# A two-layer conv/attention trunk: one depthwise block moved to VectorE, norms and opening loads reordered

## The chip, the cores and the metric

The kernel runs on one core of one Trainium2 chip. The metric is the device time of one execution in microseconds (us). A core has TensorE (matrix products; its weight loads are shown as an engine of their own), VectorE, ScalarE, GpSimd (POOL) and SyncE (SP, which here only issues DMAs). Each engine works off its own queue in order and waits on semaphores for the others.

## The reference, cut to what matters

The input is 256 tokens of 1024 channels, float32. Two layers, each with a mixer between two half-step SwiGLU FFNs: the first layer's mixer is a causal Conformer convolution, the second's a stick-breaking attention. The change sits in the first FFN's opening and in the convolution.

```python
for i in range(DEPTH):                       # 2
    x = x + 0.5 * swiglu_ffn(rms_norm(x, g[0]), ffn_w_in[i, 0], ffn_w_out[i, 0])
    h = rms_norm(x, g[1])
    x = x + (conformer_conv(h, ...) if i == 0 else stick_breaking_attention(h, ...))
    x = x + 0.5 * swiglu_ffn(rms_norm(x, g[2]), ffn_w_in[i, 1], ffn_w_out[i, 1])
return rms_norm(x, final_g)

def conformer_conv(h, ...):
    val, gate = jnp.split(h @ w_pw1 + b_pw1, 2, axis=-1)
    u = val * jax.nn.sigmoid(gate)
    u = depthwise_causal_conv(u, w_dw) + b_dw          # 31 taps, each channel by itself
    u = jax.nn.silu(layer_norm(u, ln_g, ln_b))
    return u @ w_pw2 + b_pw2
```

## The kernel before, in words

**Tiling.** The 256 tokens are two tiles of 128 (t = 0, 1); the 1024 channels are eight blocks of 128 (k = 0 to 7). Every float32 product is made of three products of two parts: an operand is split into hi (a cast by ScalarE, L142) and lo (the difference, a tensor_tensor on VectorE, L143), and `mm3` (L171) multiplies hi by hi, hi by lo and lo by hi. All weights are loaded from memory once, into one of three `raw` buffers, and split into one of six `hi` and six `lo` buffers of `ring`. A load waits until its `raw` buffer has been split; a split waits until TensorE has finished with the buffer that it takes.

**FFN** (`ffn`, L257). Eleven steps j of 256 hidden columns. Each loads a piece of `w_in` and of `w_out`. In the first FFN the first two steps (`lead` = 2) are done by `start` (L766), written out by hand; from step j = 2 on `C` (L281) makes the products with the tokens as columns, and `V` (L303) multiplies the step's result by `w_out`, one step later. Outside the stages written out by hand a planner sets the order on each engine, by estimated readiness.

**The opening** (`start`, L798 to L849) is in hand-written order for TensorE, SP, ScalarE and VectorE. SP loads x, then `w_in` for j = 0 and 1. `keep_busy` issues dummy transposes on TensorE. `turn_x`, `gain` and `split_x` bring x into the operand layout, `cast(j, k)` splits one row block of the weights (`lo` on VectorE, or on POOL where `nc.gpsimd` is passed), `mm` issues the products. After it the planner takes over; SP fetches `w_out` for j = 0 and j = 1 before `w_in` for j = 2, in the order of the loop at L352.

**The convolution** (`conv`, L385 to L611) is in hand-written order too.
- `U(e, t)` (L426) makes 24 products for the column pair e (blocks 2e and 2e + 1, value and gate) of token tile t. After its third step (k = 2) it runs `finish()`, the gate that the U before it left pending, and then what else it was given. At its end ScalarE scales the result into `vg` (L434).
- The pending gate (L436) transposes `vg` on TensorE (L439), and for each of its two blocks ScalarE takes a sigmoid (L442) and VectorE multiplies (`up`, L443). Then `shifted` (L468) issues four DMAs for the block, which make four copies shifted by one token each (`sk`).
- `weights(e)` (L454) builds the tap matrices of two blocks on VectorE, one instruction for each.
- `taps(k, tb, nt)` (L478) does the 31 taps of block k as 32 small matrix products on `sk` (64 instructions in the trace), with `finish()` in the middle; ScalarE then adds the bias into `acc[k]` (L490).
- `norm_in(t, q)` (L496) transposes four blocks of `acc` back and takes `bn_stats`; `norm(t)` (L506) makes the layer norm and the SiLU of one token tile: VectorE, POOL (rstd), VectorE, ScalarE (sigmoid), VectorE, for two halves. `turn(t, q)` (L525) transposes the result and splits it; `out_mm(t, n)` (L533) makes 24 products with `conv_w_pw2`.
- The order is L552 to L610. In the second half all taps of tile 0 are followed by those of tile 1; `norm(0)` lies between the taps of tile 1, `norm(1)` behind out_mm's first products.

Of the kernel before, what the change touches and what calls it, by code (L numbers as in the profile page):

```python
# [14 lines left out]
P = 128  # L15
# [17 lines left out]
def trunk_kernel(  # L33
# [55 lines left out]


# [8 lines left out]
    def load_conv_consts():  # L99
# [121 lines left out]
    def u_mm(t, units, between=None):  # L221
        ps = ps_u.tile([P, 512], F32, tag="u", name=nm("psu"))
        for k in range(KD):
            u_step(ps, t, k, units)
            if between is not None and k == 2:
                between()
        return ps

    def u_cm(units):
# [10 lines left out]
        u = wk.tile([P, T, P], F32, tag="A", bufs=13, name=nm("u"))  # L240
# [4 lines left out]
    def row_rstd(hTs):  # L245

        pr = ps_t.tile([P, T, P], F32, tag="tr", name=nm("pr"))
        for t in range(T):
            rb = wk.tile([P, P], F32, tag="A", bufs=13, name=nm("rb"))
# [7 lines left out]
    def ffn(i, f, gi, hTs, next_gi, first=None, start=None, hook=None, final=False):  # L257
# [3 lines left out]
        def gate(t, j, ps):  # L261
            rstd = hTs[t][2]
            s = wk.tile([P, 256], F32, tag="A", bufs=13, name=nm("s"))
            nc.scalar.activation(s, ps[:, 0:256], AF.Sigmoid, scale=rstd)
            p = wk.tile([P, 256], F32, tag="A", bufs=13, name=nm("p"))
            nc.vector.scalar_tensor_tensor(p, ps[:, 0:256], rstd, s, op0=ALU.mult, op1=ALU.mult)
            a = wk.tile([P, 256], F32, tag="A", bufs=13, name=nm("a"))
# [13 lines left out]
        def C(j, units, rrow):  # L281

            hs, ls = [], []
            for q in range(2):
                for c in range(2):
                    u = u_cm([w[:, :, c, q * P : (q + 1) * P] for w in unit] for unit in units)
                    if c == 0:
                        nc.vector.tensor_tensor(u, u, rrow, op=ALU.mult)  # L288
                        a = wk.tile([P, T, P], F32, tag="A", bufs=13, name=nm("s"))
# [60 lines left out]
        outs = [None, None]  # L350
        prev = None
        for j in range(NJ):  # L352
# [4 lines left out]
            vu = load_rows(w_out, 2 * j)  # L357
# [10 lines left out]
            if j == NJ - 1:  # L368
                V(0, j - 1, prev)
                V(1, j - 1, prev, (0,))  # L370
                V(0, j, vu)
                outs[0] = end(0)
                V(1, j - 1, prev, (1,))
                V(1, j, vu)
                outs[1] = end(1)
            elif j:
                for t in range(T):
                    V(t, j - 1, prev)
            prev = vu
# [5 lines left out]
    def conv(hTs, next_gi, next_w):  # L385
# [40 lines left out]
        def U(e, t, *todo):  # L426
# [5 lines left out]
            ps = u_mm(t, units[e], between=between)  # L432
# [3 lines left out]
            def gate():  # L436
# [3 lines left out]
                for q, k in enumerate((2 * e, 2 * e + 1)):  # L440
# [8 lines left out]
                    elif t == T - 1:  # L449
                        shifted(k, 0, SW)  # L450
# [17 lines left out]
        def shifted(k, a, b):  # L468

            if k not in sks:  # L470
                sks[k] = wk.tile([P, 4, SW], F32, tag="sk", bufs=4, name=nm("sk"))
            for g in range(4):
                v = up[k][32 * g : 32 * g + 32, a:b]
                nc.sync.dma_start(
# [3 lines left out]
        def taps(k, tb, nt, pool, tag):  # L478
# [13 lines left out]
            )  # L492

# [39 lines left out]
        def out_mm(t, n):  # L533
            ns = slice(n * 512, (n + 1) * 512)
            pv = ps_v.tile([P, 512], F32, tag=f"v{t}{n}", name=nm("psv"))
            for k in range(KD):
# [4 lines left out]
                )  # L541
            nc.vector.tensor_tensor(xt[t][:, ns], pv, xt[t][:, ns], op=ALU.add)

        for _ in range(KD):
            up.append(wk.tile([P, H + T * P], F32, tag="A", bufs=13, name=nm("up")))
# [5 lines left out]
        with tc.manual_schedule(engines={E.PE, E.SP, E.Activation, E.DVE}):  # L551
# [11 lines left out]
            U(1, 0, (weights, 0), (cast, units[2][0]))  # L563
# [50 lines left out]
    def attention(hTs, next_gi):  # L614
# [9 lines left out]
        ones = wk.tile([P, WS], F32, tag="sk", bufs=4, name="ones")  # L624
# [260 lines left out]
```

## Time and profile before

| | |
|---|---|
| median of 3 runs | 998.3 us (998.02 to 998.73) |
| the profiled execution | 1000.22 us, of which the span from its first to its last instruction is 998.4 us |
| TensorE busy | 983.9 us, 99% of the span |
| VectorE busy | 709.2 us, 71% |
| ScalarE busy | 514.5 us, 52% |
| POOL busy | 134.8 us, 14% |
| the chain that ended last | TensorE 93%, VectorE 3%, ScalarE 2% |

TensorE's share is an average over all stages. What is to be read from it is only where TensorE is not busy, and who was waited for there. Times in the rows are microseconds from the span's start.

### The profile page before, as it was taken

To read this page: it belongs to the slowest core of one execution; us is meant where nothing else is said; L and a number is where in the kernel's file an instruction comes from. 1 tells how busy PE (TensorE), PEld (TensorE's weight loads), DVE (VectorE), ACT (ScalarE), POOL (GpSimd) and SP (SyncE) were. 2 spreads that over 40 slices of the span, in tenths; PEclk is the share of its full clock that TensorE was granted. 3 is DMA by queue.
4 is the path that set the end of the run, shared out by engine and by line. 5 is a ranking of instruction groups with operands and counts; after the bars stand their busy time and mean duration, and the time that the engine had idled before them with its cause. 6 is when DMAs were issued, how large, how long until landed. Compare 5 with 4: busy or idle time off the path is not lost.

```text
span 998.4 us, 14842 instructions
## 1 busy us (share of the span) xinstructions
PE 983.9 (99%) x5727; PEld 817.7 (82%) x5727; DVE 709.2 (71%) x1092; ACT 514.5 (52%) x872; POOL 134.8 (14%) x169
## 2 busy tenths in 40 slices
PE   9999999999989999999999999999999999999997
PEld 7788888886778888888888888888777788888885
DVE  5876776754777776767777676767777986767654
ACT  6654545353536454545554545455554355555532
POOL 3011111100011111111121111111101011111111
PEclk9999999999999999999999999999999999999999
DMA  7867564536735756565557464755625255656511
GB/s 254 293 218 247 179 223 154 169 105 225 220 123 174 229 169 211 166 213 162 176 170 225 154 222 158 217 163 169 210 90 166 91 163 169 212 168 210 170 43 43
DMA packets 143175, 177.76 MB, mean 178 GB/s; under 512 B 6456, under 2 KB 126336, under 8 KB 143104
## 3 DMA queue, kind: packets, MB, share of 16 engines
q1 hardware_dynamic: 142752, 176.26, 54.9%
q8 instruction: 45, 0.74, 0.3%
q10 hardware_dynamic: 352, 0.55, 0.2%
q14 instruction: 26, 0.21, 0.1%
HBM read 171.08 MB, written 1.05 MB: 172 GB/s over the span
## 4 chain that ended last, share of the span: by engine, by line
PE 93%; DVE 3%; ACT 2%; issue 1%; DMA 1%; POOL 0%; POOLq 0%; SPq 0%; ACTq 0%; DVEq 0%
PE psc L236 28%; PE psc L237 16%; PE psv L172 8%; PE psv L173 8%; PE psv L174 8%; PE psc L239 4%; PE psu L172 4%; PE psu L173 4%; PE psu L174 4%; PE pc L484 2%; DVE lo L143 1%; PE ptr L194 1%; PE pz L662 1%; ACT hi L142 1%; PE pwo L172 1%
## 5 line engine op out<-in xcount | busy, mean ns | idle before, releaser
L143 DVE TENSOR_TENSOR lo<-raw,hi 128x1024 fp32r<-128x1024 f32 (+1 forms) x358 | 397.3, 1133 | 81.8 <-ACT hi L142 81.4
L236 PE MATMUL psc<-xT,hi 128*128 128x512 f32 x1204 | 433.2, 398 | 1.7 <-ACT hi L142 1.7
L142 ACT CAST hi<-raw 128x1024 fp32r<-128x1024 f32 (+1 forms) x360 | 327.4, 952 | 89.3 <-PE psc L236 32.4
L237 PE MATMUL psc<-xT,lo 128*128 128x256 f32 x1376 | 358.7, 281 | 0.0
L237 PEld LDWEIGHTS psc<-xT,lo 128*128 128x128 f32 x1376 | 259.9, 189 | 15.7 <-issue 0.4
L236 PEld LDWEIGHTS psc<-xT,hi 128*128 128x128 f32 x1204 | 226.6, 188 | 50.7 <-ACT hi L142 2.0
L292 POOL TENSOR_TENSOR s<-s,rrow 128x256 f32<-128x256 f32 x78 | 90.8, 1164 | 585.5 <-DVE s L291 583.6
L172 PE MATMUL psv<-hi,ah 128*128 128x512 f32 x352 | 138.3, 393 | 0.1
L173 PE MATMUL psv<-lo,ah 128*128 128x512 f32 x352 | 138.0, 392 | 0.0
L174 PE MATMUL psv<-hi,al 128*128 128x512 f32 x352 | 136.8, 390 | 0.0
L241 ACT COPY u<-psc 128x256 f32<-128x256 f32 x172 | 63.7, 370 | 130.6 <-PE psc L239 130.5
L242 DVE TENSOR_TENSOR u<-psc,u 128x256 f32<-128x256 f32 x172 | 72.2, 420 | 77.6 <-ACT u L241 76.9
L142 ACT CAST ah<-s 128x256 fp32r<-128x256 f32 x78 | 31.7, 407 | 94.6 <-DVE s L294 94.6
L173 PEld LDWEIGHTS psv<-lo,ah 128*128 128x128 f32 x352 | 66.5, 189 | 14.0
L172 PEld LDWEIGHTS psv<-hi,ah 128*128 128x128 f32 x352 | 66.4, 189 | 13.5 <-ACT ah L142 1.3
L174 PEld LDWEIGHTS psv<-hi,al 128*128 128x128 f32 x352 | 66.0, 188 | 13.8
L172 PE MATMUL psu<-hi,xT 128*128 128x512 f32 x176 | 70.1, 398 | 0.0
L173 PE MATMUL psu<-lo,xT 128*128 128x512 f32 x176 | 69.1, 393 | 0.1
L174 PE MATMUL psu<-hi,xT 128*128 128x512 f32 x176 | 68.8, 391 | 0.0
L239 PE MATMUL psc<-xT,hi 128*128 128x512 f32 x172 | 68.4, 398 | 0.0
L290 ACT ACTIVATE s<-u 128x256 f32<-128x256 f32 x78 | 32.4, 415 | 45.6 <-DVE u L288 45.6
L143 DVE TENSOR_TENSOR al<-s,ah 128x256 fp32r<-128x256 f32 x78 | 32.7, 419 | 21.7 <-ACT ah L142 21.7
(129 smaller groups left out, 798.5 us busy)
## 6 DMA issues: line engine op xcount, KB each, us to landing
raw<-in_ffn_w_in_dram SPq DMA_DIRECT2D x168, 512.0 KB, 4.8
raw<-in_ffn_w_out_dram SPq DMA_DIRECT2D x44, 1024.0 KB, 5.0
raw<-in_conv_w_pw_dram SPq DMA_DIRECT2D x16, 512.0 KB, 4.5
raw<-in_attn_w_qkv_dram SPq DMA_DIRECT2D x16, 512.0 KB, 4.8
raw<-in_ffn_w_in_dram SPq DMA_DIRECT2D x16, 256.0 KB, 5.2
raw<-in_conv_w_pw_dram SPq DMA_DIRECT2D x4, 1024.0 KB, 6.6
raw<-in_attn_w_qkv_dram SPq DMA_DIRECT2D x4, 1024.0 KB, 5.2
raw<-in_attn_w_o_dram SPq DMA_DIRECT2D x4, 1024.0 KB, 4.8
```

What stands on the lines that cost most here:

```text
L142: copy(hi, src)
L143: (eng or nc.vector).tensor_tensor(lo, src, hi.bitcast(F32), op=ALU.subtract)
L172: nc.tensor.matmul(ps, lh, rh, start=start, stop=False)
L173: nc.tensor.matmul(ps, lh, rl, start=False, stop=False)
L174: nc.tensor.matmul(ps, ll, rh, start=False, stop=stop)
L236: nc.tensor.matmul(ps, h, xT[:, :, k, :, :], start=k == 0, stop=False)
L237: nc.tensor.matmul(ps[:, :, 0, :], l, xT[:, :, k, 0, :], start=False, stop=False)
L239: nc.tensor.matmul(ps, h, xT[:, :, k, :, :], start=False, stop=True)
L241: nc.scalar.copy(u, ps[:, :, 1, :])
L242: nc.vector.tensor_tensor(u, ps[:, :, 0, :], u, op=ALU.add)
L290: nc.scalar.activation(a, u, AF.Sigmoid)
L292: nc.gpsimd.tensor_tensor(a, a, rrow, op=ALU.mult)
```

## The change

What it does:
- **Block 0 on VectorE.** `taps(0, ...)` goes from TensorE. `taps_dve` does the 31 taps of block 0 as 31 VectorE instructions over 128x256 that accumulate in `acc[0]`, with a per-partition weight from `wd`; they are issued in seven groups of 5, 5, 3, 6, 3, 6 and 3. The shifted copies and the tap matrix of block 0 are no longer made. `wd` is loaded and transposed in `load_conv_consts`.
- **Order of the convolution's second half.** `taps(2)` and `taps(3)` come behind U(3,0), then `weights(3)`, then the taps of tile 0 for blocks 4 to 7, and only then U(3,1), which carries `norm_in` and `norm` of tile 0 from its first step on (`at=0`). The taps of tile 1 come between `turn(0, ...)` and the products of tile 0; `norm(1)` is started in the first step of out_mm(0,1).
- **DMAs.** The shifted copies of block 7 are issued by ScalarE instead of SP.
- **The opening.** Eight dummy transposes instead of ten ahead of `turn_x(1)`, and none instead of ten ahead of the first product; the `lo` of row block 0 moves from POOL to VectorE and that of row block 1 from VectorE to POOL. In the first FFN `w_out` of j = 1 is loaded at j = 2, behind `w_in` of j = 2.
- **Buffers.** Tag A has 10 instead of 13 slots, tag sk 5 instead of 4.

```diff
+    wd = const.tile([P, TAPS], F32, name="wd")
...
+        wrow = wk.tile([TAPS, P], F32, tag="sg", name="wrow")
+        load(wrow, conv_w_dw[0, :, :P])
+        ps = ps_t.tile([P, 512], F32, tag="tr", name="pst_wd")
+        nc.tensor.transpose(ps[:, :TAPS], wrow, ident[:TAPS, :TAPS])
+        nc.vector.tensor_copy(wd, ps[:, :TAPS])
...
-    def u_mm(t, units, between=None):
+    def u_mm(t, units, between=None, at=2):
...
-            if between is not None and k == 2:
+            if between is not None and k == at:
...
-            vu = load_rows(w_out, 2 * j)
+            if j == 0 or j >= lead:
+                vus += [load_rows(w_out, 2 * c) for c in range(len(vus), j + 1)]
...
-                    elif t == T - 1:
+                    elif t == T - 1 and k:
                         shifted(k, 0, SW)
...
-            for i in range(2):
+            for i in range(2) if e else (1,):
                 k = 2 * e + i
...
-                nc.sync.dma_start(
+                (nc.scalar if k == 7 else nc.sync).dma_start(
...
+        def taps_dve(a, b):
+
+            for tau in range(a, b):
+                src, w = up[0][:, tau + 1 : tau + 1 + T * P], wd[:, tau : tau + 1]
+                if tau == 0:
+                    nc.vector.tensor_scalar(acc[0], src, w, vec[:, BD : BD + 1], op0=ALU.mult, op1=ALU.add)
+                else:
+                    nc.vector.scalar_tensor_tensor(acc[0], src, w, acc[0], op0=ALU.mult, op1=ALU.add)
...
-        def out_mm(t, n):
+        def out_mm(t, n, *todo):
...
+                if k == 0:
+                    for f, *args in todo:
+                        f(*args)
...
-            U(1, 0, (weights, 0), (cast, units[2][0]))
+            U(1, 0, (weights, 0), (cast, units[2][0]), (taps_dve, 0, 5))
...
-            U(1, 1, (cast, units[2][1]))
+            U(1, 1, (cast, units[2][1]), (taps_dve, 5, 10))
             fetch_out(0)
-            taps(0, 0, T, ps_v, "v01")
-            U(2, 0, (weights, 1), (cast, units[3][0]))
+            U(2, 0, (weights, 1), (cast, units[3][0]), (taps_dve, 10, 13))
             fetch_out(1)
             taps(1, 0, T, ps_v, "v11")
-            U(2, 1, (cast, units[3][1]))
+            taps_dve(13, 19)
+            U(2, 1, (cast, units[3][1]), (taps_dve, 19, 22))
             fetch_out(2)
-            taps(2, 0, T, ps_v, "v01")
+            taps_dve(22, 28)
             U(3, 0, (weights, 2), (cast, vunits[0]), (cast, vunits[1]))
             fetch_out(3)
             nxt.append(fetch_chunk(next_w, 0, DFF, 0))
+            taps(2, 0, T, ps_v, "v01")
+            taps_dve(28, TAPS)
             taps(3, 0, T, ps_v, "v11")
-            U(3, 1, (weights, 3), (cast, vunits[2]))
-            nxt.append(fetch_chunk(next_w, 0, DFF, 1))
+            weights(3)
             taps(4, 0, 1, ps_v, "v01")
-            norm_in(0, 0)
-            cast(vunits[3])
+            cast(vunits[2])
             taps(5, 0, 1, ps_v, "v11")
             for t in range(T):
                 nc.vector.tensor_tensor(xt[t], xt[t], b2, op=ALU.add)
-            taps(6, 0, 1, ps_u, "u")
-            taps(7, 0, 1, ps_u, "u")
+            taps(6, 0, 1, ps_v, "v01")
+            taps(7, 0, 1, ps_v, "v11")
+
+            U(3, 1, (norm_in, 0, 0), (norm_in, 0, 1), (norm, 0), (cast, vunits[3]), at=0)
+            nxt.append(fetch_chunk(next_w, 0, DFF, 1))
+            taps(4, 1, 1, ps_u, "u")
+            turn(0, 0)
+            taps(5, 1, 1, ps_u, "u")
+            turn(0, 1)
             cast(nxt[0])
-            taps(4, 1, 1, ps_u, "u")
-            norm_in(0, 1)
-            norm(0)
-            taps(5, 1, 1, ps_u, "u")
+            out_mm(0, 0)
+            taps(6, 1, 1, ps_u, "u")
             norm_in(1, 0)
-            taps(6, 1, 1, ps_u, "u")
-            turn(0, 0)
             taps(7, 1, 1, ps_u, "u")
-            turn(0, 1)
-            norm_in(1, 1)
-            norm(1)
-            out_mm(0, 0)
-            cast(nxt[1])
-            out_mm(0, 1)
+            out_mm(0, 1, (norm_in, 1, 1), (norm, 1))
             for q in range(2):
                 turn(1, q)
+            cast(nxt[1])
             out_mm(1, 0)
...
-            keep_busy(10)
+            keep_busy(8)
             pts = [turn_x(1, q) for q in range(2)]
-            cast(0, 0, nc.gpsimd)
+            cast(0, 0)
             xgs = [gain(pts[0], 0, 0)]
-            cast(0, 1)
+            cast(0, 1, nc.gpsimd)
             xgs.append(gain(pts[1], 0, 1))
             split_x(1, 0, xgs[0])
-            keep_busy(10)
             mm(0, (0, 0))
```

In the diff every `bufs=13` of tag A becomes `bufs=10` and every `bufs=4` of tag sk becomes `bufs=5`; `V` and `end` take their `w_out` from the list `vus`.

## Rows read from the trace of the kernel before

**Rows 1.** The page's first section: busy us, share and instructions of each engine.

```profile
PE 983.9 (99%) x5727; PEld 817.7 (82%) x5727; DVE 709.2 (71%) x1092; ACT 514.5 (52%) x872; POOL 134.8 (14%) x169
```

**Rows 2.** TensorE's waits: line waited <- releaser: us in total, times, longest.

```profile
PE pc L484 <- ACT acc L490: 1.8, 1, 1.8
PE psc L236 <- ACT hi L142: 1.7, 1, 1.7
...
PE ptr L529 <- DVE m L522: 0.8, 1, 0.8
```

**Rows 3.** Timeline of TensorE in the convolution: start, us, line, out<-in, count.

```profile
214.26 0.60 PE L439 MATMUL ptr<-ident,vg 128*128 128x128 f32 x4
214.62 0.48 PE L172 MATMUL psu<-hi,xT 128*128 128x512 f32 x1
...
224.14 1.93 PE L484 MATMUL pc<-sk,wb 128*32 128x256 f32 x32
226.00 0.66 PE L439 MATMUL ptr<-ident,vg 128*128 128x128 f32 x4
...
228.45 0.50 PE L172 MATMUL psu<-hi,xT 128*128 128x512 f32 x1
...
234.16 1.93 PE L484 MATMUL pc<-sk,wb 128*32 128x256 f32 x32
```

**Rows 4.** VectorE: three instructions of the opening, then groups (busy us, mean ns).

```profile
20.58 0.48 DVE L266 SCALAR_TENSOR_TENSOR p<-psu,rstd,s 128x256 f32<-128x256 f32 x1 [3.26 <-ACT s L264]
21.09 0.48 DVE L268 SCALAR_TENSOR_TENSOR a<-psu,rstd,p 128x256 f32<-128x256 f32 x1
21.49 0.68 DVE L143 TENSOR_TENSOR lo<-raw,hi 128x512 fp32r<-128x512 f32 x1
...
L242 DVE TENSOR_TENSOR u<-psc,u 128x256 f32<-128x256 f32 x172 | 72.2, 420 | 77.6 <-ACT u L241 76.9
...
L520 DVE SCALAR_TENSOR_TENSOR z<-z,lnr,lnb 128x512 f32<-128x512 f32 x4 | 3.0, 752 | 0.4 <-POOL lnr L180 0.3
L517 DVE SCALAR_TENSOR_TENSOR z<-pl,mv,fg 128x512 f32<-128x512 f32 x4 | 3.0, 748 | 0.1
```

**Rows 5.** Timeline of VectorE in the convolution; in brackets the idle time before.

```profile
216.41 2.35 DVE L459 TENSOR_TENSOR wb<-ind,wq 128x1024 f32<-128x1024 f32 x2
218.68 2.50 DVE L143 TENSOR_TENSOR lo<-raw,hi 128x512 fp32r<-128x512 f32 x4
...
247.20 0.35 DVE L443 SCALAR_TENSOR_TENSOR up<-ptr,vec,sg 128x128 f32<-128x128 f32 x1 [5.08 <-ACT sg L442]
```

**Rows 6.** Timeline of ScalarE around U(3,0).

```profile
247.58 0.37 ACT L442 ACTIVATE sg<-ptr,vec 128x128 f32<-128x128 f32 x1 [0.42 <-DVE up L443]
...
249.00 3.89 ACT L142 CAST hi<-raw 128x1024 fp32r<-128x1024 f32 x4
254.30 0.69 ACT L434 ACTIVATE vg<-psu,rstd 128x512 f32<-128x512 f32 x1 [1.42 <-PE psu L174]
```

**Rows 7.** Timeline of VectorE and ScalarE: both ends of norm(0).

```profile
276.25 0.69 DVE L503 BATCH_NORM_STATS2 st<-pl 128x6 f32<-128x512 f32 x1
...
281.81 0.63 ACT L521 ACTIVATE m<-z 128x512 f32<-128x512 f32 x1 [2.27 <-DVE z L520]
```

**Rows 8.** DMA issues by line: ns min/median/max of one issue.

```profile
L474 SPq DMA_DIRECT2D sk<-up x40: 543/603/1507, 215.8 to 272.3; - x40
...
L341 ACTq DMA_DIRECT2D out_dram<-o x2: 338/354/369, 990.9 to 995.0; - x2
```

**Rows 9.** First FFN: ScalarE, TensorE, and a window of 1 us (clock after POOL).

```profile
29.34 2.00 ACT L142 CAST hi<-raw 128x1024 fp32r<-128x1024 f32 x2 [2.43 <-DMA raw<-in_ffn_w_out_dram]
...
34.38 0.73 PE L236 MATMUL psc<-xT,hi 128*128 128x512 f32 x2 [1.72 <-ACT hi L142]
...
36.50:37.50 1.00, 1.00 (x4) 0.81 (x3) 1.00 (x3) 0.63 (x1) 0.00 (x0) 0.50 0.70 287
```

**Rows 10.** Timeline of TensorE in the opening.

```profile
11.72 0.49 PE L173 MATMUL psu<-lo,xT 128*128 128x512 f32 x1
```

More of the change, by code (lines that the diff above doesn't have):

```diff
@@ L239, in u_cm @@
                 nc.tensor.matmul(ps, h, xT[:, :, k, :, :], start=False, stop=True)
-        u = wk.tile([P, T, P], F32, tag="A", bufs=13, name=nm("u"))
+        u = wk.tile([P, T, P], F32, tag="A", bufs=10, name=nm("u"))
         nc.scalar.copy(u, ps[:, :, 1, :])
@@ L248, in row_rstd @@
         for t in range(T):
-            rb = wk.tile([P, P], F32, tag="A", bufs=13, name=nm("rb"))
+            rb = wk.tile([P, P], F32, tag="A", bufs=10, name=nm("rb"))
             nc.gpsimd.tensor_copy(rb, hTs[t][2].broadcast_to([P, P]))
@@ L288, in C @@
                         nc.vector.tensor_tensor(u, u, rrow, op=ALU.mult)
-                        a = wk.tile([P, T, P], F32, tag="A", bufs=13, name=nm("s"))
+                        a = wk.tile([P, T, P], F32, tag="A", bufs=10, name=nm("s"))
                         nc.scalar.activation(a, u, AF.Sigmoid)
@@ L349, in ffn @@
         ]
-        outs = [None, None]
-        prev = None
+        outs, vus = [None, None], []
         for j in range(NJ):
@@ L368, in ffn @@
             if j == NJ - 1:
-                V(0, j - 1, prev)
-                V(1, j - 1, prev, (0,))
-                V(0, j, vu)
+                V(0, j - 1, vus[j - 1])
+                V(1, j - 1, vus[j - 1], (0,))
+                V(0, j, vus[j])
                 outs[0] = end(0)
-                V(1, j - 1, prev, (1,))
-                V(1, j, vu)
+                V(1, j - 1, vus[j - 1], (1,))
+                V(1, j, vus[j])
                 outs[1] = end(1)
@@ L377, in ffn @@
                 for t in range(T):
-                    V(t, j - 1, prev)
-            prev = vu
+                    V(t, j - 1, vus[j - 1])
             if j == 5 and hook:
@@ L424, in finish, with U @@
                 pending.pop()()
-        def U(e, t, *todo):
+        def U(e, t, *todo, at=2):
             def between():
@@ L430, in between @@
                     f(*args)
-            ps = u_mm(t, units[e], between=between)
+            ps = u_mm(t, units[e], between=between, at=at)
             vg = wk.tile([P, 4, P], F32, tag="B", bufs=4, name=nm("vg"))
@@ L470, in shifted @@
             if k not in sks:
-                sks[k] = wk.tile([P, 4, SW], F32, tag="sk", bufs=4, name=nm("sk"))
+                sks[k] = wk.tile([P, 4, SW], F32, tag="sk", bufs=5, name=nm("sk"))
             for g in range(4):
                 v = up[k][32 * g : 32 * g + 32, a:b]
-                nc.sync.dma_start(
+                (nc.scalar if k == 7 else nc.sync).dma_start(
                     sks[k][:, g, a:b], bass.AP(tensor=v.tensor, offset=v.offset, ap=[v.ap[0], [1, 4], [1, b - a]])
@@ L541, in out_mm @@
                 )
+                if k == 0:
+                    for f, *args in todo:
+                        f(*args)
             nc.vector.tensor_tensor(xt[t][:, ns], pv, xt[t][:, ns], op=ALU.add)
         for _ in range(KD):
-            up.append(wk.tile([P, H + T * P], F32, tag="A", bufs=13, name=nm("up")))
+            up.append(wk.tile([P, H + T * P], F32, tag="A", bufs=10, name=nm("up")))
             nc.gpsimd.memset(up[-1][:, :H], 0.0)
@@ L623, in attention @@
         WS = W0 + W1
-        ones = wk.tile([P, WS], F32, tag="sk", bufs=4, name="ones")
+        ones = wk.tile([P, WS], F32, tag="sk", bufs=5, name="ones")
         nc.gpsimd.memset(ones, 0.0)
@@ L629, in attention @@
         for i in range(2):
-            nb = wk.tile([P, WS], F32, tag="sk", bufs=4, name=f"nb{i}")
+            nb = wk.tile([P, WS], F32, tag="sk", bufs=5, name=f"nb{i}")
             nc.gpsimd.memset(nb, 0.0)
@@ L674, in scores @@
                 nc.scalar.activation(be, pz, AF.Sigmoid, scale=scale)
-                sc = wk.tile([P, WS], F32, tag="A", bufs=13, name=nm("scan"))
+                sc = wk.tile([P, WS], F32, tag="A", bufs=10, name=nm("scan"))
                 nc.vector.tensor_tensor_scan(
@@ L678, in scores @@
                 )
-                a = wk.tile([P, 3, P], F32, tag="A", bufs=13, name=nm("aa"))
+                a = wk.tile([P, 3, P], F32, tag="A", bufs=10, name=nm("aa"))
                 nc.vector.tensor_tensor(a[:, 0, :], be[:, 0, :], sc[:, 1 : P + 1], op=ALU.mult)
@@ L692, in transpose_a @@
                     nc.tensor.transpose(pa[:, c, :], a[:, c, :], ident)
-                aT = wk.tile([P, 3, P], F32, tag="A", bufs=13, name=nm("aT"))
+                aT = wk.tile([P, 3, P], F32, tag="A", bufs=10, name=nm("aT"))
                 nc.vector.tensor_copy(aT, pa)
```

6 lines of the change are left out of this document (3 added, 3 removed).

## The prediction

> **What bounds the kernel now.** I read the engine line first: TensorE is busy 983.9 of the span's 998.4 us, VectorE 71%, ScalarE 52% [rows 1]. So time is lost only where TensorE does work that can go, or where it waits. Its waits come next: after the opening's first 1.7 us three stand out. In the convolution a tap product waits 1.8 us for ScalarE and a transpose 0.8 us for VectorE; in the first FFN the first C product waits 1.7 us for a hi cast [rows 2]. The change works at exactly these places. The third view is the timeline of the convolution, engine by engine, since its four queues run in the order in which the code is written: what stands behind a late instruction is late with it.
>
> **What is removed from TensorE.** `taps(0)` runs from 224.14 to the next product at 228.45, 4.31 us; the gate's transposes inside it (226.00) stay, but between products they take 0.36 (214.26 to 214.62) [rows 3]. With 0.4 for them that is 3.9 us; the transposes of gate(2,1) make the same move, from between taps to between products, for 0.2. Sum -4.1 us, all on the path. The waits of [rows 2] in the convolution are to go too: 1.8 + 0.8 = -2.6.
>
> **What VectorE gets.** 31 taps over 128x256. The nearest row is the gate's scalar_tensor_tensor of that shape with a per-partition scalar: 0.48 us. Its dependent successor starts 0.51 after it (20.58 to 21.09), an independent one 0.40 after (21.09 to 21.49) [rows 4]. Each tap reads the `acc` that the tap before wrote, so I take 0.51: 31 x 0.51 = 15.8 us. The upper bound is 0.55. The lower one is a tensor_tensor of that width, 0.42, overlapped by 0.08 as above: 0.34 [rows 4]. That taps read SBUF only doesn't help by the rows: the same operation at 512 wide takes 748 ns with a PSUM source and 752 ns from SBUF alone [rows 4]. The Trainium skill, "VectorE: DVE Perf Modes", section "The TRN2 errata", has a table by which an SBUF source costs 58 cycles and a PSUM source 120, beside one cycle for each element; by that a tap would be an estimated 0.33 us and the chain 10 us. The 4 ns between the two rows don't show that table's difference of some 65 ns.
>
> **Does it fit?** I lay VectorE's operations one behind another from 216.41, where it begins the first `weights` [rows 5]. Up to gate(2,1) its queue holds: three `wb` at 1.13 = 3.4 (half of `weights(0)` is gone); sixteen lows, 2.50 for four less the overlap, = 9.8 [rows 5]; three gates at about 1.06 = 3.2 (two `up` of 0.35 with ScalarE's next sigmoid between them) and 0.3 of waiting; 28 taps = 14.3. Sum 31: it is free at about 247.0. When is it wanted? TensorE still reaches the end of U(1,1) at 224.1 [rows 3]. A U is 24 products, 5.5 to 5.7 (228.45 to 234.16) [rows 3]. Then: U(2,0) with transposes 5.9, the first half of taps(1) 1.9, transposes and second half 2.5, U(2,1) 5.5, three steps of U(3,0) 2.1, and a wait of 0.5 in taps(1) (ScalarE is late there by the same mechanism): 242.3. Transposes and sigmoid follow, and `up` is wanted at 243.2. VectorE is 3.8 us late. Before, it sat idle 5.08 us ahead of this same `up` [rows 5]: the taps use that up, and more.
>
> **Who waits for that.** ScalarE. Its second sigmoid follows the first `up`; behind it stand four hi casts of `w_pw2` (3.89 us), then `vg` of U(3,0) (0.69) [rows 6]. With `up` at 247.0: sigmoid to 247.7, casts to 251.5, `vg` to 252.2. TensorE has finished U(3,0) at 246.0 and the first half of taps(2) at 247.8, and then wants that `vg` to transpose: **wait 4.4 us**. Even with VectorE in time 0.6 of it would stay: gate(2,1) stood half a tap block ahead of U(3,0) and stands inside it now, so ScalarE has 4 us less.
>
> **The norm behind U(3,1).** `norm(0)` now starts after step 0 of U(3,1). From the second `bn_stats` to the end of the second sigmoid took 276.25 to 282.44 = 6.2 us [rows 7]; `cast(vunits[3])` (two casts, 1.9) and then `vg` of U(3,1) (0.7) are queued behind it on ScalarE: 8.8 us. TensorE has seven steps (4.8) and half a block of 128-wide taps (1.0) to do: 5.8. **Wait 3.0 us** at the transposes of gate(3,1). `norm(1)` likewise: 6.2 and VectorE's product of 0.7, against seven steps of out_mm(0,1) and four transposes, 5.3: **wait 1.7** at turn(1,1).
>
> **The DMAs moved to ScalarE.** The shifted copies of block 7 are issued by ScalarE, four for each token tile. An issue takes 0.60 us on SP; ScalarE's own issues take 0.35, of another transfer [rows 8]. I take 0.60, the same transfer: 2.4 us each time in which ScalarE does nothing else. The first time `acc` of taps(2) is behind it, and with it the PSUM bank that taps(4) wants: **0.6**. The second time the hi half of turn(0,0): **1.3** at out_mm(0,0). With 0.35 these are 0 and 0.5. The Trainium skill, "DMA: Bandwidth & Descriptors", section "Issuing engines are not separate DMA queues", says that issuing from more engines only saves sequencer time; no run here shows the copies issued by ScalarE. SP's queue gets shorter by twelve issues, worth nothing here: TensorE waits for none of them.
>
> Waits added: 0.5 + 4.4 + 0.6 + 3.0 + 1.3 + 1.7 = 11.5. The convolution: -4.1 - 2.6 + 11.5 = **+4.8**.
>
> **TensorE's clock.** After the gap of 1.72 us before 34.38 the granted clock fell to 0.50, which is 1.2 GHz, for three windows of 1 us from 35.5 to 38.5 (one stands): 1.5 us lost [rows 9]. Two of the new waits are longer than that gap, so up to 2 x 1.5 = 3.0; but a slower TensorE fills 1.9 of the waits that come behind (0.6 and 1.3). I take **+1.1**, bounds 0 and 3.
>
> **The opening.** Before, `w_out` of j=1 is fetched ahead of `w_in` of j=2, ScalarE waits 2.43 us for it and casts it first (29.34), and the first C product starts at 34.38 [rows 9]. Exchanged, `w_in` has that place: its first cast is done by 30.4, and the gap of 1.72 goes with the 1.5 of clock behind it, except for a rest that I put at 0.3, because the second half of the unit lands just when it is wanted. **-2.9**, bounds 0 and -3.2. At the very start the stream without gaps begins with the product at 11.72 [rows 10], held by a VectorE low; VectorE's low of step 0 moves into its idle ahead of the gain and what follows comes 0.3 earlier: **-0.3**. That fewer dummy transposes let the clock fall there is a risk of +1.5.
>
> **The rest.** Load and transpose of `wd`: +0.2 at most. Slots of A from 13 to 10: nothing in the FFNs, where a step holds six; the attention holds eight to ten, bounds 0 and +2, and I take 0; fewer slots release nothing earlier, so there is no gain in it.
>
> Sum: 4.8 + 1.1 - 2.9 - 0.3 + 0.2 = **+2.9 us**. The profiled execution took 1000.2, 1.8 above its span and 1.9 above the median of 998.3 (998.02 to 998.73); it becomes 1003.1, and the median **1001.2**.
>
> **Rivals.** (a) VectorE keeps up, because a tap costs 0.34 to 0.40. The 4.4 becomes 0.6 to 1.9, the 0.5 goes, and the clock costs half: 3.0 to 4.8 less, **996.4 to 998.2**. For it: VectorE's idle time in this stage, and the independent pair at 0.40; against it: the dependent pair at 0.51. The table named above would give this case. (b) The other side: the cover holds. If ScalarE reaches `vg` of U(3,1) within 5.8 us of the second `bn_stats`, and `up` of gate(2,1) comes in time, the waits of 4.4, 3.0, 1.3 and 1.7 go, and the clock's loss: 998.3 - 4.1 - 2.6 - 3.2 + 1.2 = **990**. It decides at whether that chain can be shorter than 6.2 us; the row of before says no. (c) The opening gives nothing, because `w_in` lands no sooner or the clock falls with fewer dummies: **1004.4**. (d) Fewer slots stall the attention: **1003.2**.
>
> **Chances.** Forecast 0.50, its own range 999.5 to 1003.5; (a) 0.20; (b) 0.12; (c) 0.12; (d) 0.06. The range leaves out (b) and a tail above: **996 to 1005**. A measurement of this kernel tells 0.2%, 2 us, from no change. Faster: (b) and the lower third of (a), 0.18. Same: the rest of (a) and the lower end of the forecast, 0.24. Slower: 0.58.
>
> **What would show it.** In the profile after: the tap products of 64 instructions fewer; a VectorE line of 31 instructions about 0.51 apart; the transposes of `vg` waiting for ScalarE about 4 us in taps(2) and about 3 us after U(3,1), with a granted clock below 1 behind one of them; no gap at the first C product. The prediction is wrong if VectorE has idle time ahead of gate(2,1), or if TensorE's waits in the convolution sum to less than 7 us.

## The result, and the profile after

The changed kernel takes **1009.2 us** (1006.9 to 1010.9), 1.0109 times the kernel before (95% interval 1.0085 to 1.0132): 11 us more, where 2.9 was forecast, and outside the range. The profiled execution is the fastest of its runs, 1006.85 us with a span of 1005.1. That is 6.6 us over the profiled execution of before; the medians lie 4.4 us further apart, since that execution was 2.1 above its median and this one is 2.3 below. Its page, engine line and granted clock in tenths by 40 slices:

```profile
PE 982.7 (98%) x5652; PEld 816.0 (81%) x5652; DVE 723.1 (72%) x1123; ACT 513.7 (51%) x871; POOL 135.5 (13%) x169
...
PEclk9999999999999999999999999999999999999999
```

Against [rows 1] VectorE is 14 us busier (31 taps) and TensorE nearly as busy as before, though 64 tap products and twelve dummy transposes are gone: part of its work ran at a lower clock, for which the slices are too wide. TensorE's waits, as in [rows 2]:

```profile
PE ptr L444 <- ACT vg L439: 7.0, 2, 3.9
PE ptr L543 <- DVE m L536: 1.9, 1, 1.9
PE pc L489 <- ACT acc L495: 1.8, 1, 1.8
```

TensorE's timeline, the lines that answer to [rows 9] and [rows 3], then the convolution's four waits:

```profile
32.06 0.48 PE L242 MATMUL psc<-xT,hi 128*128 128x512 f32 x1
...
205.73 0.60 PE L444 MATMUL ptr<-ident,vg 128*128 128x128 f32 x4
...
249.26 1.11 PE L444 MATMUL ptr<-ident,vg 128*128 128x128 f32 x4 [3.91 <-ACT vg L439]
250.30 7.83 PE L489 MATMUL pc<-sk,wb 128*32 128x256 f32 x96
259.96 7.20 PE L489 MATMUL pc<-sk,wb 128*32 128x128 f32 x256 [1.83 <-ACT acc L495]
...
277.86 0.66 PE L444 MATMUL ptr<-ident,vg 128*128 128x128 f32 x4 [3.13 <-ACT vg L439]
...
302.76 0.78 PE L543 MATMUL ptr<-ident,m 128*128 128x128 f32 x4 [1.89 <-DVE m L536]
```

The first C product has no gap ahead of it, and the first gate of the convolution (205.73) comes 2.6 us earlier than the 208.35 of before. VectorE's taps (ns of one), then VectorE and ScalarE ahead of the longest wait, against [rows 5] and [rows 6]:

```profile
L506 DVE SCALAR_TENSOR_TENSOR acc<-up,wd,acc x30: 474/485/489, 217.8 to 254.0; 128x256 f32<-128x256 f32 x30
...
239.54 4.64 DVE L506 SCALAR_TENSOR_TENSOR acc<-up,wd,acc 128x256 f32<-128x256 f32 x9
244.10 0.35 DVE L448 SCALAR_TENSOR_TENSOR up<-ptr,vec,sg 128x128 f32<-128x128 f32 x1
...
244.74 3.87 ACT L148 CAST hi<-raw 128x1024 fp32r<-128x1024 f32 x4
248.52 0.69 ACT L439 ACTIVATE vg<-psu,rstd 128x512 f32<-128x512 f32 x1
...
254.01 5.38 ACTq L479 DMA_DIRECT2D sk<-up  x4
259.44 0.84 ACT L495 ACTIVATE acc<-pc,vec 128x256 f32<-128x256 f32 x2 [6.73 <-DMA sk<-up]
```

Nine taps stand right ahead of gate(2,1)'s `up`, which has no idle time before it now, and behind `up` come the casts and `vg`. Three windows of 1 us of TensorE, one behind each of three waits (us, busy, granted clock, DMA share, GB/s):

```profile
251.00:252.00 1.00, 1.00 (x12) 0.50 1.06 166
...
281.00:282.00 1.00, 1.00 (x28) 0.50 1.00 389
305.00:306.00 1.00, 1.00 (x4) 0.50 0.00 0
```

TensorE works there at 1.2 GHz; the clock is below 2.4 from about 248.5 to 255.7, 279.2 to 282.6 and 303.1 to 306.5.

**Three stretches.** Each profile is cut at two places, the transposes of gate(0,0) and those of the first boundary behind the convolution (starts in TensorE's timeline; "rest" is the span less the second). These three columns are of one profiled execution each, the ratio is of all runs. The runs are those of the experiments below:

| profile | first gate at | convolution | rest | ratio to before (95%) |
|---|---|---|---|---|
| before | 208.35 | 95.27 | 694.8 | 1 |
| before, again | 206.64 | 96.88 | 696.4 | 1.0000 (0.9989 to 1.0012) |
| changed | 205.73 | 104.58 | 694.8 | 1.0109 (1.0085 to 1.0132) |
| changed, again | 208.92 | 110.22 | 694.7 | 1.0107 (1.0072 to 1.0142) |
| opening alone | 205.05 | 96.89 | 694.8 | 0.9984 (0.9975 to 0.9994) |
| opening, filled | 205.93 | 95.42 | 694.7 | 0.9989 (0.9979 to 0.9999) |
| clock filled | 207.24 | 105.91 | 695.2 | 1.0087 (1.0070 to 1.0104) |
| copies on SP | 207.69 | 102.30 | 694.7 | 1.0059 (1.0044 to 1.0074) |
| SP and filled | 206.25 | 98.48 | 695.4 | 1.0016 (1.0007 to 1.0025) |
| block 0 on TensorE | 206.71 | 100.73 | 695.0 | 1.0042 (1.0028 to 1.0056) |
| taps later | 205.91 | 95.39 | 695.1 | 0.9991 (0.9981 to 1.0001) |
| reordered | 206.72 | 97.10 | 695.9 | 1.0012 (1.0001 to 1.0022) |
| reordered again | 206.32 | 94.10 | 695.7 | 0.9976 (0.9965 to 0.9987) |
| copies first | 206.21 | 90.14 | 695.8 | 0.9962 (0.9950 to 0.9974) |

The rest is the same in the changed kernel as before (694.8), so the whole loss lies in the convolution: 9.3 us in the profiled execution where 5.9 were forecast (4.8 and the clock's 1.1), and 15.0 in the second one. In the second profile of before the rest is 1.6 us longer, with the granted clock at 0.50 from about 784 to 787 us; in the three reordered kernels it is about 1 us longer without such a drop, and why was not followed up.

### The profile page after: what moved, and what is told of

It reads as the page before. It is cut to its first block, busy times and chain, and to the rows that moved or that the text cites. A ratio compares the mean times of both kernels' runs of the same rounds, so it can differ in the third digit from the quotient of the medians.

```text
span 1005.1 us, 14770 instructions
## 1 busy us (share of the span) xinstructions
PE 982.7 (98%) x5652; PEld 816.0 (81%) x5652; DVE 723.1 (72%) x1123; ACT 513.7 (51%) x871; POOL 135.5 (13%) x169
## 4 chain that ended last, share of the span: by engine, by line
PE 87%; DVE 7%; DMA 2%; ACT 2%; issue 1%; POOL 0%; SPq 0%; POOLq 0%; ACTq 0%; DVEq 0%
PE psc L242 28%; PE psc L243 16%; PE psv L178 9%; PE psv L180 8%; PE psv L179 8%; PE psc L245 4%; DVE lo L149 3%; PE psu L179 2%; PE psu L178 2%; PE psu L180 2%; PE pc L489 1%; DVE acc L506 1%; DMA raw<-in_ffn_w_in_dram 1%; PE ptr L200 1%; PE pz L678 1%
## 5 line engine op out<-in xcount | busy, mean ns | idle before, releaser
L297 DVE TENSOR_TENSOR s<-s,u 128x256 f32<-128x256 f32 x78 | 32.9, 422 | 21.1 <-ACT s L296 21.1
```

Of the source, the lines that this page charges most:

```text
L297: nc.vector.tensor_tensor(a, a, u, op=ALU.mult)
```

## The experiments

**The changed kernel again.** No edit.

> The changed kernel once more, unchanged, for a second profile and more times. Theory (the time over the profiled execution, 2.3 us at the median, is clock that falls for longer or in more places in other executions): the waits are the same within 0.2 us, and the mean granted clock goes with the span. Rival: the waits themselves differ between executions by a microsecond or more.

Its profiled execution took 1015.6 us. The waits that VectorE and the norm cause are the same to 0.1 us; the one for `acc` is 4.4 us instead of 1.8, and so the rival holds: waits differ between executions. Nor does the mean granted clock go with the span: it is 0.993 in a run of 1011.4 us and 0.992 in one of 1007.5. Waits, ScalarE's queue, and TensorE's taps behind the wait for `acc`:

```profile
PE ptr L444 <- ACT vg L439: 7.0, 2, 3.9
PE pc L489 <- ACT acc L495: 4.4, 1, 4.4
...
257.21 7.37 ACTq L479 DMA_DIRECT2D sk<-up  x4
...
265.15 10.05 PE L489 MATMUL pc<-sk,wb 128*32 128x128 f32 x256 [4.37 <-ACT acc L495]
```

The same 256 products took 7.20 us in the first profile. Here the clock fell at this wait too (below 1.00 from about 264 to 271). So of the 5.6 us that this convolution is longer, 2.5 are the wait and 2.9 the clock behind it; two smaller differences elsewhere nearly cancel.

The four copies of block 7 that ScalarE issues took 7.37 us from the first issue's start to the last one's end, 5.38 in the first profile; 2.4 was forecast. In the first profile (SP's four of block 6, ScalarE's third and fourth, a window with PE, PEld, DVE, ACT, POOL, clock, DMA share, GB/s, and ScalarE's second set):

```profile
253.09 4.91 SPq L479 DMA_DIRECT2D sk<-up  x4
...
255.90 0.55 ACTq L479 DMA_DIRECT2D sk<-up  x1
258.84 0.55 ACTq L479 DMA_DIRECT2D sk<-up  x1
...
257.00:258.00 1.00, 1.00 (x24) 0.36 (x13) 0.00 (x0) 0.00 (x0) 0.00 (x0) 1.00 1.07 366
...
280.12 2.89 ACTq L479 DMA_DIRECT2D sk<-up  x4
```

An issue takes about 0.55 us, near SP's 0.54 to 0.60 [rows 8]. The time goes in the gaps: the third issue ends at 256.45, the fourth begins at 258.84, and in between ScalarE does nothing, with the 16 DMA engines at a share of about 1.0 and SP issuing block 6's copies beside it. The eight copies together took 6.3 us on the two queues here (SP's begin at 253.09) and 8.2 in the second profile. Block 7's `up` was done at 253.09, yet ScalarE's first issue begins at 254.01, just behind the end of taps(2), whose `sk` slot block 7 takes over; in the second profile it is so too. That this slot held ScalarE for some 0.9 us is likely, but no run changed the number of slots alone.

**The clock filled.** Dummy transposes in the four waits:

```diff
+                if e == 3:
+                    fill((33, 27)[t])
                 for q in range(4):
                     nc.tensor.transpose(pt[:, q, :], vg[:, q, :], ident)
...
             weights(3)
+            fill(15)
             taps(4, 0, 1, ps_v, "v01")
...
+            turn(1, 0)
+            fill(16, "v00")
+            turn(1, 1)
```

> The changed kernel with dummy transposes of TensorE put into its four long waits (33 ahead of gate(3,0)'s transposes, 27 ahead of gate(3,1)'s, 15 ahead of taps(4), 16 ahead of turn(1,1)); the waits stay as long. Theory (the clock behind the waits is the term that was too small, about 6 us in the profiled execution): granted clock near 1 through the convolution, 1002 to 1004 us. Rival (the waits alone, or something outside of the convolution, cost what is over the forecast): no change, 1008 to 1009.

It took 1.0087, the rival's number. The clock stayed at 1.00 behind the four filled waits, but the time came back in waits that were not there or shorter before:

```profile
250.78 0.66 PE L446 MATMUL ptr<-ident,vg 128*128 128x128 f32 x4 [0.17 <-ACT vg L439]
...
262.34 7.19 PE L491 MATMUL pc<-sk,wb 128*32 128x128 f32 x256 [3.80 <-ACT acc L497]
...
286.53 0.50 PE L178 MATMUL psv<-hi,xT 128*128 128x512 f32 x1 [1.56 <-ACT xT L148]
...
254.69 7.08 ACTq L481 DMA_DIRECT2D sk<-up  x4
```

ScalarE's issues end at 261.77 here, and TensorE, done earlier, waits 3.80 us in spite of 15 dummies for what stands behind them; the second four cost 1.56 us at out_mm(0,0), near the 1.3 that was forecast for that place, with a drop of the clock behind it. What a faster clock gives is lost again where the next wait is set by something that no clock moves, so this run doesn't price the clock.

**Copies on SP.** The one thing taken back is who issues block 7's copies:

```diff
-                (nc.scalar if k == 7 else nc.sync).dma_start(
+                nc.sync.dma_start(
```

> The changed kernel with block 7's shifted copies issued by SP again. Theory (ScalarE's four issues beside SP's cost 1.8 us at the wait for acc in taps(4) and slow later work): that wait is gone, 1.8 us less, and with the clock behind it 2 to 4 us less in all: 1005 to 1007 us. Rival (the wait for acc comes from ScalarE's lateness after the casts, not from the issues): the wait stays over 1 us, 1008 to 1009.

1.0059 against 1.0107: 4.8 us less by the ratios, 3.8 by the medians of the two sets (1005.95 and 1009.79), and the interval of 1.0107 alone is 7 us wide. So it is the theory's 2 to 4 us or somewhat more. The wait for `acc` is gone. On SP alone the eight copies of blocks 6 and 7 take 7.33 us (5.7 to 8.3 in the other runs that have them there), about as long as on two queues, and nothing but copies and loads stands behind them there:

```profile
255.05 7.33 SPq L479 DMA_DIRECT2D sk<-up  x8
```

**SP and filled.** Both edits together (without `fill(15)`, whose wait is gone).

> The changed kernel with block 7's shifted copies on SP (as in the run of that name, whose convolution took 102.3 us from gate(0,0)'s transposes to those of the first boundary) and, besides, dummy transposes in the three waits that are left (3.9, 3.1 and 1.9 us). With the copies on SP no wait can grow to take what the clock gives. Theory (the clock is a term of its own, some 2.5 us here): the three waits stay, granted clock 1.00 throughout, convolution 99.5 to 100, time 2 to 3 us under the copies on SP alone, a ratio to before of about 1.003 to 1.004. Rival (a clock drop is hidden behind the next wait and costs nothing): convolution 102.3, ratio 1.006.

1.0016 against 1.0059, the convolution 98.48 against 102.30. Windows of TensorE from 230 us to about the end of the convolution (clock after the count), first with the copies on SP alone, then filled:

```profile
230.00:312.00 82.00, 72.26 (x902) 0.94 0.51 153
...
230.00:305.00 75.00, 73.39 (x943) 1.00 0.51 151
...
260.49 4.32 PE L491 MATMUL pc<-sk,wb 128*32 128x128 f32 x128 [1.27 <-DMA sk<-up]
```

With the waits of 3.9, 3.1 and 1.9 us kept, and TensorE merely kept at work in them, 3.8 us come back (4.3 by the ratios). The mean granted clock bears this out in all runs: 0.997 to 0.999 here, 0.991 to 0.995 without the dummies. But that a wait could not grow here was wrong: at taps(6) TensorE waits 1.27 us for the shifted copies (the last line), where the run without dummies shows 0.77 idle at about the same place. So 3.8 is what the clock costs in these three places less some 0.5 that this wait took back.

**Taps later.** Copies on SP, and taps 20 to 30 behind gate(3,0):

```diff
-            taps_dve(13, 19)
-            U(2, 1, (cast, units[3][1]), (taps_dve, 19, 22))
+            taps_dve(13, 17)
+            U(2, 1, (cast, units[3][1]), (taps_dve, 17, 20))
             fetch_out(2)
-            taps_dve(22, 28)
...
-            taps_dve(28, TAPS)
+            taps_dve(20, 24)
             taps(3, 0, T, ps_v, "v11")
             weights(3)
+            taps_dve(24, TAPS)
```

> The changed kernel with block 7's copies on SP, and eleven of VectorE's 31 taps (20 to 30) moved behind gate(3,0); eight of them stood ahead of gate(2,1). Theory (VectorE's queue is what makes vg of U(3,0) late): the wait of 3.9 us falls to 0.6, the clock stays up there (1.5 us), the other waits (3.1, 1.9) stay: convolution 97 to 98 against 102.3, ratio to before about 1.001. Rival (the wait is ScalarE's four casts of w_pw2, which stand ahead of vg in any case): the wait stays over 2.5 us, convolution 101 to 102, ratio 1.005.

0.9991: 6.8 us less than with the copies on SP alone, and level with the kernel before. VectorE at gate(2,1), TensorE's waits, and the clock of the whole convolution:

```profile
240.71 0.35 DVE L448 SCALAR_TENSOR_TENSOR up<-ptr,vec,sg 128x128 f32<-128x128 f32 x1 [0.53 <-ACT sg L447]
...
245.88 0.66 PE L444 MATMUL ptr<-ident,vg 128*128 128x128 f32 x4 [0.38 <-ACT vg L439]
...
256.46 1.80 PE L489 MATMUL pc<-sk,wb 128*32 128x128 f32 x42 [1.11 <-DVE acc L506]
...
272.09 0.66 PE L444 MATMUL ptr<-ident,vg 128*128 128x128 f32 x4 [3.13 <-ACT vg L439]
...
295.07 0.63 PE L543 MATMUL ptr<-ident,m 128*128 128x128 f32 x4 [1.89 <-DVE m L536]
...
206.00:302.00 96.00, 89.20 (x1007) 1.00 0.55 168
```

VectorE is in time again (0.53 us idle), the wait of 3.9 is 0.38, and ScalarE's casts, the rival, are not what made it. The waits of 3.13 and 1.89 are unchanged, as the theory has it, yet the clock stayed at 1.00 behind both: here a wait of 3.1 us did not drop it, and in the changed kernel one of 1.9 did. So of the 6.9 us that the convolution is shorter, 3.5 are the wait and most of the rest is clock, more than the 1.5 of the theory. This profile has the highest mean granted clock of its ten runs (0.999; the lowest is 0.995), so others lost more to it. The wait of 1.11 at taps(6) is put down to VectorE's taps, on which those products do not depend; in two other runs with the copies on SP the wait there is for the copies (1.27 above, 0.80 in the next run).

**Block 0 on TensorE.** The new order alone, copies on SP:

```diff
             fetch_out(0)
+            taps(0, 0, T, ps_v, "v01")
-            U(2, 0, (weights, 1), (cast, units[3][0]), (taps_dve, 10, 13))
+            U(2, 0, (weights, 1), (cast, units[3][0]))
...
```

> The new order alone: block 0's taps are on TensorE again, as a second tap block between U(1,1) and U(2,0), and block 7's copies on SP. Theory (the move to VectorE gives TensorE 4.1 us and takes about 5 at the wait for vg): 4.1 us more products, the wait of 3.9 gone with the clock behind it, the waits of 3.1 and 1.9 still there since they come from the order: convolution 101 to 102, ratio to before 1.003 to 1.006. Rival (the move itself is a clean gain and the loss lies in the order alone): convolution 106, ratio 1.010.

1.0042, as the theory has it; the convolution, 100.73, is just under its range. The wait at gate(3,0) is 0.4 without a tap on VectorE, and the waits of 3.1 and 1.9 are there, so they belong to the order and not to the taps. Against the run with later taps TensorE has 5.3 us more; some 1.5 of it is a clock drop behind the 3.1 us wait (the transposes and taps behind it take 6.0 us, 4.5 there), so 3.8 is the block itself, for which 4.1 was forecast.

**Opening alone, and filled.** The kernel before with the hunks of the opening, and then with dummies in its convolution's two waits:

```diff
+            fill(6)
             turn(0, 0)
+            fill(15)
             taps(7, 1, 1, ps_u, "u")
```

> The kernel before with the opening's part of the change alone (loads exchanged, first casts moved, fewer dummy transposes). By the sum on record the opening is worth 2.9 + 0.3 = 3.2 us: 995.1 us. If all of the opening's gain were lost again later (rival c): 998.3.

> The kernel before with the opening's part of the change alone and, besides, dummy transposes in the two waits of its convolution (0.8 and 1.8 us). Theory (the opening is worth some 3 us, and the first run of the opening alone showed 1.3 because the 1.8 us wait dropped the clock behind it, 1.6 us): convolution 95.3 with the clock at 1.00, time 1 to 1.6 us under the opening alone, ratio to before 0.996 to 0.9975. Rival (the opening's gain is smaller in most executions, since it hangs on when the loads land): ratio 0.998 to 0.999, with first gate transposes at 207 or later.

0.9984 and 0.9989: the opening brings 1.6 and 1.1 us (intervals 0.6 to 2.5 and 0.1 to 2.1), not 3.2, and the filling nothing that could be measured. The second run's ratio is its rival's, though its first gate is not (205.93). In the profiles the filled waits leave the clock at 1.00 and the convolution at 95.42, where it was 96.89 with a drop; the next run shows that the drop is not in every execution.

**Before again.** No edit.

> The kernel before, unchanged, for a second profile. Theory (its 1.8 us wait for acc sometimes drops the clock and sometimes not, which is why its executions differ by several us): the waits of 0.8 and 1.8 us are there as in the first profile; the granted clock behind them is at either level, and the convolution takes 95.3 us, or 96.9 with the drop. Rival: the waits themselves differ by over 0.5 us.

TensorE at the first C product and at the wait for `acc`, and a window behind the latter:

```profile
33.76 0.73 PE L236 MATMUL psc<-xT,hi 128*128 128x512 f32 x2 [0.77 <-ACT hi L142]
...
281.05 2.95 PE L484 MATMUL pc<-sk,wb 128*32 128x128 f32 x64 [1.77 <-ACT acc L490]
...
282.00:283.00 1.00, 1.00 (x28) 0.50 0.07 16
```

The wait of 1.77 is the same to the hundredth; the clock behind it, at 1.00 in the first profile, is at 0.50 here and costs 1.6 us (96.88 against 95.27). And the gap at the first C product, 1.72 us with a drop behind it in the first profile [rows 9], is 0.77 here with no drop: the convolution begins at 206.64 and not at 208.35.

**Reordered, in three steps.** First: taps later, copies on SP, the casts of `w_pw2` behind `vg`, the second half of norm(0) behind gate(3,1), blocks 6 and 7 of tile 1 inside out_mm(0,0).

```diff
-            U(3, 0, (weights, 2), (cast, vunits[0]), (cast, vunits[1]))
+            U(3, 0, (weights, 2))
+            cast(vunits[0])
+            cast(vunits[1])
...
+            cast(vunits[3])
+            U(3, 1, (norm_in, 0, 0), (norm_in, 0, 1), (norm_a, 0, 0), (norm_a, 0, 1), (norm_b, 0, 0), at=0)
             taps(4, 1, 1, ps_u, "u")
+            norm_b(0, 1)
...
+            out_mm(
+                0, 0, (3, taps, 6, 1, 1, ps_u, "u"), (3, norm_in, 1, 0), (3, taps, 7, 1, 1, ps_u, "u"),
+                (4, norm_in, 1, 1), (4, norm, 1),
+            )
```

> A kernel after the measured waits: taps as in the run with later taps, copies on SP, the casts of w_pw2 behind vg, the second half of norm(0) behind gate(3,1), blocks 6 and 7 of tile 1 and norm(1) inside out_mm(0,0), turn(1,1) inside out_mm(1,0). Theory (the change's idea is right, TensorE gets 4.1 us, and the waits come from where the work stands in the queues): waits in the convolution sum to 3 us at most, no drop of the clock, convolution 90 to 91.5 against 95.3 of before, with the opening 992 to 995. Rival (a queue is full whatever the order, and each wait taken away comes back behind another engine): waits of over 6 us in sum, convolution 95 or more, 998 to 1001.

1.0012, the rival's number. ScalarE and TensorE around U(3,1):

```profile
266.33 2.01 ACT L148 CAST hi<-raw 128x1024 fp32r<-128x1024 f32 x2 [3.47 <-PE psu L180]
...
274.22 0.81 PE L444 MATMUL ptr<-ident,vg 128*128 128x128 f32 x4 [4.20 <-ACT vg L439]
```

The cast of `vunits[3]` waited 3.47 us for products of U(3,1) that hold its slot, held ScalarE, and the norm with it. The second step puts it behind turn(0,1), `cast(vunits[1])` behind gate(3,0), and turn(1,0) into out_mm(0,1); it also puts `cast(vunits[0])` back ahead of `vg` and the addition of `b2` back to its place in the changed kernel.

> The reordered kernel, with the casts that stood in the way in the profile of the first one put elsewhere: cast(vunits[3]) behind turn(0,1) (it waited for a slot that U(3,1) frees and held ScalarE), cast(vunits[1]) behind gate(3,0), turn(1,0) inside out_mm(0,1). Theory (waits come from places in a queue): no wait over 1.5 us in the convolution, 3 us in sum, clock at 1.00, convolution 89 to 91, ratio to before 0.992 to 0.995. Rival (a queue is full whatever the order): a wait of 3 us or more stays, convolution 94 or more, ratio 0.998 or more.

0.9976, between the two; the convolution (94.10) and a wait of over 3 us are the rival's. The old wait is gone, and another has come: SP, and TensorE at taps(6).

```profile
252.29 0.93 SPq L402 DMA_DIRECT2D raw<-in_ffn_w_in_dram  x2
253.32 5.66 SPq L479 DMA_DIRECT2D sk<-up  x8
...
259.87 5.65 PE L489 MATMUL pc<-sk,wb 128*32 128x128 f32 x128 [4.53 <-DMA sk<-up]
```

`up` of block 7 was done at 248.2, but the copies stood on SP behind a load that waits for the raw slot of `vunits[1]`, cast later now. Third step:

```diff
-            nxt.append(fetch_chunk(next_w, 0, DFF, 0))
             taps(2, 0, T, ps_v, "v01")
+            nxt.append(fetch_chunk(next_w, 0, DFF, 0))
```

> The second reordered kernel with one load moved: the first half of the next FFN's w_in, whose issue waits on SP for the raw slot that cast(vunits[1]) frees, stands behind the shifted copies of blocks 6 and 7 instead of ahead of them. Theory (the wait of 4.5 us at taps(6) is SP's queue: the copies stood behind that load from 248.1 to 252.3): the copies are issued some 4 us earlier, the wait falls under 1 us, no drop of the clock, convolution 88.5 to 90, ratio to before 0.991 to 0.994. Rival (the copies themselves take that long, 16 DMA engines being busy): a wait of over 2 us stays, convolution 92 or more, ratio 0.996 to 0.998.

**0.9962** (995.7 us; before 999.1 beside it), the fastest of all by its ratio, though its interval overlaps that of the second step. The ratio is the rival's (0.996 to 0.998), the profile is near the theory's. SP, TensorE's longest waits, and the convolution's clock:

```profile
247.41 8.28 SPq L479 DMA_DIRECT2D sk<-up  x8
...
255.56 3.59 PE L489 MATMUL pc<-sk,wb 128*32 128x128 f32 x109 [0.27 <-DMA sk<-up]
...
268.89 0.66 PE L444 MATMUL ptr<-ident,vg 128*128 128x128 f32 x4 [1.02 <-ACT vg L439]
...
206.00:297.00 91.00, 89.36 (x1007) 1.00 0.57 173
```

In the profile the wait at taps(6) is 0.27, the waits sum to 1.6 us, the clock is at 1.00 and the convolution takes 90.14, just over the theory's 90 and 5.1 us shorter than the first of before. The median gains only 3.5: the twelve runs go from 993.8 to 999.5, and the profiled one (993.9) is among the three fastest. Its mean granted clock is 0.999, that of the slowest 0.994. An estimate from these two (0.005 of the span) is some 5 us lost to the clock, most of what the slowest loses; where it fell was not profiled. The rest behind the convolution is 1.0 longer than before (table).

## Why the prediction was wrong, point by point

**What held.** A tap takes 485 ns and follows the last by 0.51 us: four take 2.04, as forecast from the dependent pair of [rows 4]. So VectorE has no idle time ahead of gate(2,1), where the prediction would have been wrong by its own sign, and rival (a) falls. The table of the Trainium skill that stood behind it ("VectorE: DVE Perf Modes", section "The TRN2 errata", an estimated 0.33 us) doesn't hold for this instruction; the section says itself that the row it comes from is too low for single operations. Nor did the other sign come: the waits in the convolution sum to 10.8 us (forecast 11.5). VectorE's terms add up to 247.4, not to the 247.0 that the prediction goes on with; `up` began at 244.10, in a convolution that starts 2.6 earlier. `vg` of U(3,0) was waited for 3.9 us (forecast 4.4), `vg` of U(3,1) 3.1 (3.0), turn(1,1) 1.9 (1.7); the wait of 0.5 in taps(1) did not come. TensorE got some 3.8 us from block 0 (4.1). The slots of A, rival (d), show no cost: the rest of the span is 694.8 in both.

**First failed step: the DMAs moved to ScalarE.** "An issue takes 0.60 us on SP; ... I take 0.60" took the length of one issue for the time of four. [rows 8] holds lengths only; its longest, 1507 ns, was a hint. The trace of before held more, since SP's eight copies of two blocks stand there from first to last:

```profile
257.63 6.20 SPq L474 DMA_DIRECT2D sk<-up  x8
```

That is 0.78 us for each and some 3 us for four, where 2.4 was taken. In the changed kernel four took 5.4 to 7.4 us at that place, and 2.9 the second time (from 280.12). The Trainium skill ("DMA: Bandwidth & Descriptors", section "Issuing engines are not separate DMA queues") says that DMAs from any engine run on the same 16 DMA engines and that issuing from several saves only sequencer time. The runs agree that a second queue adds nothing (eight copies took 6.3 to 8.2 us on two queues, 5.7 to 8.3 on one), and here not even time on the sequencers was saved. The forecast was 0.6 us of wait for `acc`; it was 1.8 and 4.4, and the run with the copies on SP puts the whole step at 4.8 us by the ratios and 3.8 by the medians, where 0.6 + 1.3 was forecast.

**Second: the clock.** "I take +1.1, bounds 0 and 3." Two drops of 1.5 were counted for two long waits, and 1.9 of that was written off against the waits behind. There were three drops, and behind the first the clock was at half for some 7 us, twice as long as in [rows 9]. With the copies on SP the three cost 3.8 us, some 0.5 of wait not counted.

Together, from gate(3,0) on, in the profiled execution: its transposes to the start of taps(4) took 10.70 us, of which 6.2 are work at full clock by the lengths of [rows 3], and 0.6 was given for the wait; that is 3.9 over. Of the 4.5 beyond the work 1.8 is the wait and some 2.7 the clock. The stretch behind gate(3,1)'s transposes took 6.1 against 4.5 without a drop, and that behind turn(1,1)'s 7.5 against 6.2 (run with later taps): 1.6 and 1.3. In place of 0.6 + 1.3 + 1.1 = 3.0 these are 4.5 + 1.6 + 1.3 = 7.4, some 4 us over; the two waits that came out 0.5 shorter each give one back. The excess in the convolution is 3.4.

The run with the copies on SP and the clock filled checks this. Without the two terms (0.6 + 1.3, and 1.1) the sum on record gives 998.2 us; with the opening at the 1.1 to 1.6 that was measured, in place of 3.2, it gives 999.8 to 1000.3. That run is at 1.0016 times before, which on the 998.2 of the result is 999.8 (interval 998.9 to 1000.7).

**Third: the opening.** The mechanism is right: no gap, no drop, the first C product at 32.06. Its size, 3.2 us, was that of one execution of before. In the other profiled one the gap is 0.77 us with no drop, and timed by itself the opening brings 1.1 to 1.6. What the new order gives also varies: the convolution begins between 205.05 and 208.92 in the twelve profiles that have it.

**The rivals.** (b) decided at whether the norm's chain could be hidden; in this kernel it could not, but the last run shows that the order can be changed so that it nearly is (a wait of 1.0 at gate(3,1), none at turn(1,1)), at 995.7 us and not at 990. (c) is half true. What weighed most, issues that stall and drops of the clock, was no rival: it was in the text as two terms, with bounds that were too narrow: 0 to 0.6 and 0.5 to 1.3 us for the two sets of issues, 0 to 3 for the clock.

**What stays open.** What sets the gaps between issues: a DMA share of about 1.0 goes with gaps of 2.4 us at 256.45 and with the short set at 280.12 alike. Why a wait of 1.8 us drops the clock in one execution and not in the next, and 3.1 us in one kernel and not in another. The changed kernel's executions differ by up to 8.7 us; the two profiled ones are the fastest and the slowest, 3.2 us apart at the first gate and 5.6 in the convolution, the latter by the wait for `acc` and the clock behind it. The others were not profiled.

## What to carry to other kernels

A DMA issue put on an engine that computes costs that engine the gaps between issues too: read it from the queue's timeline, first start to last end, and not from the length of one issue. Work moved to an idle engine pays only where each queue it stands in still meets its due times; moving eleven of 31 taps behind one gate took 6.8 us off, about half of it clock. Before sizing a gap, look at a second execution: a gap that loads make, and the clock behind any gap, may be those of one execution.

## What the runs showed of the hardware

- A second issuing queue did not speed up small copies: at the same place of the convolution 5.7 to 8.3 us for eight on SP alone, 6.3 to 8.2 for four on SP and four on ScalarE at the same time, though one issue is busy for 0.55.
- The same wait of 1.77 us, in the same kernel, left the granted clock at 1.00 in one execution and was followed by 0.50 for some 3 us in another.
- With TensorE kept at work by dummy transposes, the clock stayed at 1.00 where it had fallen behind waits of 3.9, 3.1 and 1.9 us (mean over the run 0.997 to 0.999 in ten runs, 0.991 to 0.995 in four without them).
- A chain of scalar_tensor_tensor instructions over 128x256 float32, each reading the last one's output, ran at 485 ns each and 0.51 us from one start to the next.
